# A smaller descriptor area for GpSimd's DMAs in a hybrid attention and Strassen feed-forward layer: 8 KB in place of 16 KB

## Chip, cores, metric

The kernel runs on one core of one Trainium2 chip. The metric is the device time of one execution in microseconds (us); the median of a few runs is given. A profiled execution has a span (first to last instruction) that is a little shorter than its device time.

## What is computed

One layer of a streaming encoder on x of 2048 rows by 1024 columns, float32:

```
h = rmsnorm(x, ln1_w);  proj = h @ w_in
o_diff = diff_attention(dq, dk, dv, lam, ...)    # 4 heads, 128-row query blocks, chunk-causal
o_hgrn = hgrn2(hq, hf, hi, hg, lb, ...)          # 4 heads, chunks of 64 rows, a state is carried
x = x + concat([o_diff, o_hgrn]) @ w_out         # 1024 x 1024
x = x + (silu(conv3(u)) * v) @ w_down            # u, v = rmsnorm(x, ln2_w) @ w_up, width 2816
```

## The kernel before

All matrix products with weights are made from halves: an operand is split into a rounded high part and the rest, and three matmuls (high by high, high by low, low by high) are summed in PSUM. The program has four stages.

**Mixer** (to L530). Four passes s over heads, one attention head and one HGRN head in each; a pass walks over eight blocks b of 256 rows. The steps of a block (projections, attention, HGRN) are written out by the string ORDER. Attention of a 128-row query block (`attn`, L350) goes over the keys in segments of up to 1024 for two components c: scores `sc` (L368, L369) on TensorE (PE), the row maximum `nm` (L376) on VectorE (DVE), the exponential `p` (L387) on ScalarE (ACT). There is one `sc` buffer, so the next scores wait for the exponential before. `attn_o` (L396) combines the two components (L414, DVE), transposes p (`tpa`, L420), copies it (`aT`, L422) and multiplies by the values (`av`, L425). HGRN (`hgrn`, L436) has seven levels, each with a matmul `lt` (L454) between DVE operations. A result of 128 rows goes to DRAM: `od` from `oo` (L434, attention) or from `o` (L499, HGRN). The last pass ends with the attention of query blocks 14 and 15 and the HGRN of the last 256 rows, with no projection left beside them.

**Output projection** (L533 to L626). First w_out is loaded in eight slices of 128 rows (`raw`, L546), rounded (`wo`, L548, ACT) and its rest computed (L549, GpSimd for even slices, DVE for odd). Then 16 tiles i of 128 rows: `load_o` loads the mixer's rows `ot` (L556) and x (`xt`, L558), transposes `ot` on PE (`tpo`, L564) and splits it (`oT`: L569 ACT, L570 DVE); 48 matmuls make `pjo` in two halves of 24 (L613 to L615); `xt` is added (L616), stored (L617), normalized (L620 to L622) into `ht`, which `tail` transposes (`tph`, L582) and scales for the next stage:

```
WO = []
for kt in range(ND):
    raw = rw.tile([P, D], F32, name="raw", tag="raw")
    dma(out=raw, in_=w_out[kt * P:(kt + 1) * P, :])
    w = wp.tile([P, 2, D], F32R, name=f"wo{kt}")
    ACT.copy(w[:, 0], raw)
    (POOL if kt in WOP else DVE).tensor_tensor(out=w[:, 1], in0=raw, ...)
...
def load_o(i):
    ot = wk.tile([P, D], F32, name="ot", tag="ot")
    dma(out=ot, in_=o_d[i])
```

**Up** (L633 to L736) and **down** (L739 to L881) are the two products of the feed-forward part, each by Strassen-Winograd with seven products of half size. In the down stage the partial sums of three of four groups are added to `x2d` in DRAM by accumulating DMAs that GpSimd issues (L830), 48 in all; all other DMAs are issued by SyncE's queue (SP).

**What sets the order.** The code above is traced once; a scheduler at compile time then writes a fixed order for each engine, and every engine and the SP queue carry theirs out strictly in it, waiting on semaphores. A tile may be given out only when what lay at its place is released. So the place of the buffers decides which instructions may be moved ahead of which.

**Where the buffers lie.** Each partition has one stack of pools from the bottom and one from the top. At the bottom lies the descriptor area of GpSimd's DMAs (16,384 bytes), then constants and the raw buffers `rw`, up to byte 35,840. The mixer's pool `wp` (w_in, 57,344 bytes) lies from there to 93,184; of its pools from the top the lowest is `hp` (two `hT` of 16,384 bytes, 94,208 to 126,976), above it `pp` and `sm` (small statistics, from 133,120). The next stage starts again at 35,840: `wp2` (eight `wo` of 8,192 bytes, 65,536) to 101,376, then `wk2` (`ot`, two `xt`, four `oT`, `ht`; 32,768 bytes) to 134,144. So the eighth `wo` and `ot` lie on `hT`, `oT` and `ht` on `hT` and `pp`, and the end of `ht` on the statistics of `sm`, which attention uses to its end.

The function that the diff touches:

## Time and profile before

| | before |
|---|---|
| median of 3 runs (lowest, highest) | 2782.8 us (2782.5, 2784.72) |
| profiled execution: its own time | 2783.16 us |
| its span; mean granted clock of PE | 2781.4 us; 0.985 |
| PE busy (matmul) | 2650.1 us, 95% |
| DVE, ACT, GpSimd (POOL) busy | 1900.0, 1263.6, 1051.6 us |
| DMA issued by GpSimd (q0) | 25.17 MB in 6912 packets |

Busy time is the union of an engine's instructions; matmuls overlap each other, so the distance from one start to the next says more of their cost than their duration. "Idle before" is the time for which an engine had nothing to run, put down to the instruction whose end let it go on. [...]

### The profile page before, as it was taken

The page shows a single profiled execution, that of the slowest core. Times are in us where ns is not written, and L with a number is a line of the kernel's source. Part 1 is how long each engine was busy: PE and PEld are TensorE (multiplying, and loading weights), DVE is VectorE, ACT ScalarE, POOL GpSimd, SP SyncE. Part 2 cuts the span into 40 slices and gives each one's busy share as a digit, 9 for nine tenths or more (in the row PEclk, how much of TensorE's full clock was granted, in tenths as well). Part 3 has the DMA queues.
Part 4 walks back from the last instruction along what each step waited for, and adds up shares of the span by engine and source line. Part 5 has one row for each costly group of instructions (what it writes and reads, how often), then busy time and mean ns, then how long its engine had stood idle before and what let it go on. Part 6 is the DMA issues. An engine that isn't in the chain of part 4 may idle for free. (4 is left out here: it accounts for less than half of the span.)

```text
span 2781.4 us, 42701 instructions
## 1 busy us (share of the span) xinstructions
PE 2650.1 (95%) x14722; PEld 2305.0 (83%) x14722; DVE 1900.0 (68%) x4058; ACT 1263.6 (45%) x3095; POOL 1051.6 (38%) x1168
## 2 busy tenths in 40 slices
PE   7998999999999999969999999999999998899999
PEld 6888899989999999958887888887888886687887
DVE  4677756676568656762327666669777778977787
ACT  4555644564456445542334434445344344434332
POOL 3221222212222222220325334433443446887775
PEclk9999999999999999979999999999999999999999
DMA  5323422242223232124765222225222224775754
GB/s 183 118 106 111 131 85 88 80 131 86 85 84 96 98 115 78 30 64 156 237 205 157 84 76 91 84 76 185 81 91 75 85 91 119 166 163 132 178 172 169
DMA packets 273492, 322.92 MB, mean 116 GB/s; under 512 B 19470, under 2 KB 238974, under 8 KB 269182
## 3 DMA queue, kind: packets, MB, share of 16 engines
q1 hardware_dynamic: 266366, 295.04, 32.4%
q0 software_dynamic: 6912, 25.17, 5.3%
q8 instruction: 117, 1.92, 0.3%
q14 instruction: 97, 0.79, 0.1%
HBM read 198.50 MB, written 104.86 MB: 109 GB/s over the span
## 5 line engine op out<-in xcount | busy, mean ns | idle before, releaser
L697 PE MATMUL q<-xT,WS 128*128 128x512 f32 x704 | 274.5, 390 | 2.6 <-ACT xT L630 2.6
L698 PE MATMUL q<-xT,WS 128*128 128x512 f32 x704 | 274.8, 390 | 2.2 <-DVE xT L631 2.1
L699 PE MATMUL q<-xT,WS 128*128 128x512 f32 x704 | 274.4, 390 | 0.0
L811 PE MATMUL pd<-TW,SG 128*128 128x512 f32 x616 | 244.9, 398 | 19.7 <-DVE acc L817 6.4
L813 PE MATMUL pd<-TW,SG 128*128 128x512 f32 x616 | 242.7, 395 | 3.3 <-DVE SG L631 3.3
L812 PE MATMUL pd<-TW,SG 128*128 128x512 f32 x616 | 244.0, 396 | 1.0 <-DVE TW L631 0.7
L630 ACT CAST WS<-st 128x512 fp32r<-128x512 f32 x176 | 108.5, 618 | 245.0 <-PE q L699 230.3
L697 PE MATMUL q<-xB,WS 128*128 128x512 f32 x528 | 206.9, 392 | 1.3 <-ACT xB L630 1.3
L698 PE MATMUL q<-xB,WS 128*128 128x512 f32 x528 | 206.8, 392 | 1.4 <-DVE xB L631 1.4
L699 PE MATMUL q<-xB,WS 128*128 128x512 f32 x528 | 206.6, 392 | 0.9 <-DVE WS L631 0.9
L387 ACT ACTIVATE p<-sc,nm 128x1024 f32<-128x1024 f32 (+4 forms) x192 | 165.5, 862 | 72.5 <-DVE nm L376 71.3
L631 POOL TENSOR_TENSOR WS<-st,WS 128x512 fp32r<-128x512 f32 x44 | 87.8, 1997 | 281.4 <-ACT WS L630 274.6
L376 DVE TENSOR_REDUCE nm<-sc 128x1 f32<-128x1024 f32 (+4 forms) x192 | 173.9, 906 | 12.7 <-PE sc L369 10.8
L258 PE MATMUL pj<-WA,hT 128*128 128x384 f32 x512 | 177.3, 346 | 2.6 <-DVE hT L245 2.6
L260 PE MATMUL pj<-WA,hT 128*128 128x384 f32 x512 | 175.2, 342 | 0.0
L259 PE MATMUL pj<-WA,hT 128*128 128x384 f32 x512 | 174.9, 342 | 0.0
L425 PE MATMUL av<-vst,aT 128*128 128x128 f32 x1088 | 153.0, 283 | 7.6 <-ACT aT L422 7.2
L811 PEld LDWEIGHTS pd<-TW,SG 128*128 128x128 f32 x616 | 117.9, 192 | 50.0 <-DVE acc L817 7.7
L698 PEld LDWEIGHTS q<-xT,WS 128*128 128x128 f32 x704 | 132.4, 188 | 31.1 <-DVE xT L631 3.6
L697 PEld LDWEIGHTS q<-xT,WS 128*128 128x128 f32 x704 | 132.4, 188 | 30.6 <-ACT xT L630 3.1
L630 ACT CAST WS<-rawu 128x512 fp32r<-128x512 f32 x132 | 82.2, 624 | 164.2 <-PE q L699 163.6
L699 PEld LDWEIGHTS q<-xT,WS 128*128 128x128 f32 x704 | 132.4, 188 | 27.3
(415 smaller groups left out, 7889.5 us busy)
## 6 DMA issues: line engine op xcount, KB each, us to landing
hT<-hTd SPq DMA_DIRECT2D x24, 2048.0 KB, 7.8
rawu<-in_w_up_dram SPq DMA_DIRECT2D x176, 256.0 KB, 3.0
x2d<-acc POOLq DMA_DIRECT2D x48, 512.0 KB, 6.4
gd<-c SPq DMA_DIRECT2D x176, 128.0 KB, 1.9
G<-gd SPq DMA_DIRECT2D x24, 768.0 KB, 4.2
hTd<-hT SPq DMA_DIRECT2D x8, 2048.0 KB, 6.2
qT<-qh SPq DMA_DIRECT2D x256, 64.0 KB, 2.0
rawd<-in_w_down_dram SPq DMA_DIRECT2D x22, 512.0 KB, 4.1
```

The lines of the kernel that those rows point to most:

```text
L258: PE.matmul(dst, lhsT=lh, rhs=rh, start=dt == 0, stop=False)
L259: PE.matmul(dst, lhsT=lh, rhs=rl, start=False, stop=False)
L260: PE.matmul(dst, lhsT=ll, rhs=rh, start=False, stop=dt == ND - 1)
L376: DVE.tensor_reduce(out=nm, in_=sc[:, 0:w], axis=AX.X, op=ALU.max, negate=True)
L387: ACT.activation(out=p[:, 0:w], in_=sc[:, 0:w], func=AF.Exp, bias=nm, accum_out=l)
L630: ACT.copy(dst[:, 0], src)
L697: PE.matmul(dst, lhsT=w[:, 0, cs], rhs=b_[:, 0, dt], start=dt == 0, stop=False)
L698: PE.matmul(dst, lhsT=w[:, 0, cs], rhs=b_[:, 1, dt], start=False, stop=False)
L699: PE.matmul(dst, lhsT=w[:, 1, cs], rhs=b_[:, 0, dt], start=False, stop=dt == 3)
L811: PE.matmul(pd, lhsT=Sx[n][:, 0, k], rhs=w[:, 0], start=k == 0, stop=False)
L812: PE.matmul(pd, lhsT=Sx[n][:, 0, k], rhs=w[:, 1], start=False, stop=False)
L813: PE.matmul(pd, lhsT=Sx[n][:, 1, k], rhs=w[:, 0], start=False, stop=k == len(qs) - 1)
```

## The change

The program is made with a descriptor area of 8,192 bytes per partition in place of 16,384:

```
-    nc = bacc.Bacc("TRN2", target_bir_lowering=False, num_devices=1)
+    nc = bacc.Bacc("TRN2", target_bir_lowering=False, num_devices=1, dynamic_dma_scratch_size=8192)
```

Everything that stands on the bottom stack moves down by 8,192 bytes; what hangs from the top stays. The mixer's `wp` now ends at 84,992. `wp2` is 27,648 to 93,184: its eighth slice lies in the gap below `hT` (84,992 to 93,184), which the mixer does not use. `wk2` is 93,184 to 125,952 and lies on the two `hT` alone. No instruction is added or removed, but the scheduler writes another order for the end of the mixer; ahead of it, and from the `pjo` matmuls of tile 1 on (but for four of the eight `tph` of tile 0, which come ahead of them), the order is the same.

**SP queue, end of the mixer's last pass.** `od` are the mixer's stores, `raw` the slices of w_out, `ot` and `xt` the inputs of an output tile (od_97 are the rows of tile 0, od_98 those of tile 1). Before:

```order
L434 DMA od_109<-oo 128x128
L546 DMA raw<-in_w_out_dram 128x1024 x2
L499 DMA od_109<-o_16457 128x128
L546 DMA raw<-in_w_out_dram 128x1024 x2
...
L434 DMA od_111<-oo 128x128
L499 DMA od_111<-o_16803 128x128
L499 DMA od_112<-o_16826 128x128
L434 DMA od_112<-oo 128x128
L556 DMA ot<-od_97 128x1024
L558 DMA xt<-in_x_dram 128x1024 x2
L556 DMA ot<-od_98 128x1024
```

Now:

```order
L434 DMA od_109<-oo 128x128
L556 DMA ot<-od_97 128x1024
L558 DMA xt<-in_x_dram 128x1024
L546 DMA raw<-in_w_out_dram 128x1024
L558 DMA xt<-in_x_dram 128x1024
L546 DMA raw<-in_w_out_dram 128x1024
L499 DMA od_109<-o_16457 128x128
L546 DMA raw<-in_w_out_dram 128x1024
L556 DMA ot<-od_98 128x1024
L434 DMA od_110<-oo 128x128
L546 DMA raw<-in_w_out_dram 128x1024
```

The inputs of tiles 0 and 1 have moved from behind the mixer's last store to places among the last loads of w_out.

**PE, last HGRN levels and scores.** `wo_16874` is the slice wo0 of w_out, `wo_16889` wo3 and `wo_16894` wo4. Before:

```order
L454 MATMUL lt<-qP,kp 128x128 x2
L368 MATMUL sc<-kst,qT 128x512
L369 MATMUL sc<-kst,qT 128x512
L368 MATMUL sc<-kst,qT 128x512
L369 MATMUL sc<-kst,qT 128x512
L454 MATMUL lt<-qP,kp 128x128 x2
```

Now, from the second `lt` of these on:

```order
L454 MATMUL lt<-qP,kp 128x128
L613 MATMUL pjo<-wo_16889,oT 128x512
L614 MATMUL pjo<-wo_16889,oT 128x512
L615 MATMUL pjo<-wo_16889,oT 128x512
L613 MATMUL pjo<-wo_16894,oT 128x512
L368 MATMUL sc<-kst,qT 128x512
L369 MATMUL sc<-kst,qT 128x512
L368 MATMUL sc<-kst,qT 128x512
L369 MATMUL sc<-kst,qT 128x512
L614 MATMUL pjo<-wo_16894,oT 128x512
L615 MATMUL pjo<-wo_16894,oT 128x512
```

All 48 `pjo` matmuls of tile 0 (9 ahead of that `lt`, these, and so on), its 8 `tpo` and the 8 of tile 1 have moved ahead of the last `av` matmuls of the mixer, between scores, levels and transposes.

**ACT, the eighth slice.** `wo_16909` is wo7. The difference on ACT at that place:

```order
 L548 CAST wo_16904<-raw 128x1024
-L548 CAST wo_16909<-raw 128x1024
+L569 CAST oT<-tpo 128x512 x2
 L381 ACTIVATE wv<-nm,nm_16522 128x1
 L387 ACTIVATE p,l<-sc,nm_16522 128x896
+L548 CAST wo_16909<-raw 128x1024
```

The rounding of wo7 has moved behind one exponential, and the split of tile 0's `oT` stands in its place; on DVE the rest of wo7 (L549) has moved behind one row maximum in the same way.

## Rows read from the trace of the kernel before

**Rows 1.** The page, part 2: busy and granted clock in 40 slices.

```profile
PE   7998999999999999969999999999999998899999
PEclk9999999999999999979999999999999999999999
```

**Rows 2.** Stretches: length, busy per engine (x instructions), PEclk, DMA share, GB/s.

```profile
1190.00:1212.00 22.00, 11.80 (x55) 8.88 (x54) 20.37 (x43) 12.19 (x24) 10.48 (x10) 0.73 0.51 152
1212.00:1246.00 34.00, 24.31 (x135) 20.70 (x135) 19.34 (x56) 12.64 (x33) 4.13 (x6) 0.77 0.03 7
1246.00:1254.00 8.00, 1.97 (x8) 1.57 (x8) 0.96 (x3) 0.96 (x4) 0.74 (x2) 0.62 0.59 203
1254.00:1268.00 14.00, 13.40 (x52) 10.76 (x52) 2.32 (x4) 0.63 (x2) 0.00 (x0) 0.85 0.12 39
```

**Rows 3.** PE in order of time: start, length, engine, operation, [idle before, releaser].

```profile
1211.13 0.63 PE L454 MATMUL lt<-qP,kp 128*128 128x128 f32 x2
...
1214.58 0.80 PE L368 MATMUL sc<-kst,qT 128*128 128x512 f32 x1
...
1219.54 0.50 PE L368 MATMUL sc<-kst,qT 128*128 128x512 f32 x1 [0.23 <-ACT p L387]
...
1229.40 0.50 PE L368 MATMUL sc<-kst,qT 128*128 128x512 f32 x1
...
1238.15 1.94 PE L420 MATMUL tpa<-ident,p 128*128 128x128 f32 x8 [1.71 <-DVE p L414]
...
1243.61 2.05 PE L425 MATMUL av<-vst,aT 128*128 128x128 f32 x16 [0.24 <-ACT aT L422]
1251.78 1.97 PE L564 MATMUL tpo<-ident,ot 128*128 128x128 f32 x8 [6.12 <-DMA ot<-od]
...
1254.89 0.63 PE L614 MATMUL pjo<-wo,oT 128*128 128x512 f32 x1
1255.32 0.63 PE L615 MATMUL pjo<-wo,oT 128*128 128x512 f32 x1
...
1258.47 0.40 PE L614 MATMUL pjo<-wo,oT 128*128 128x512 f32 x1
1258.70 0.39 PE L615 MATMUL pjo<-wo,oT 128*128 128x512 f32 x1
...
1268.46 0.47 PE L613 MATMUL pjo<-wo,oT 128*128 128x512 f32 x1
...
1280.37 1.03 PE L564 MATMUL tpo<-ident,ot 128*128 128x128 f32 x8
```

**Rows 4.** SP queue in order of time, end of the mixer.

```profile
1183.35 0.33 SPq L434 DMA_DIRECT2D od<-oo  x1
...
1197.79 4.14 SPq L546 DMA_DIRECT2D raw<-in_w_out_dram  x2
...
1248.10 0.42 SPq L556 DMA_DIRECT2D ot<-od  x1
```

**Rows 5.** ACT (first two rows) and DVE in order of time.

```profile
1205.49 1.04 ACT L548 CAST wo<-raw 128x1024 fp32r<-128x1024 f32 x1 [2.03 <-DMA raw<-in_w_out_dram]
...
1208.34 0.99 ACT L387 ACTIVATE p<-sc,nm 128x896 f32<-128x896 f32 x1
...
1210.24 1.20 DVE L549 TENSOR_TENSOR wo<-raw,wo 128x1024 fp32r<-128x1024 f32 x1
...
1217.03 1.22 DVE L376 TENSOR_REDUCE nm<-sc 128x1 f32<-128x1024 f32 x1
```

**Rows 6.** GpSimd's DMAs: parts 3 and 6, its costliest lines, one stretch.

```profile
q0 software_dynamic: 6912, 25.17, 5.3%
...
x2d<-acc POOLq DMA_DIRECT2D x48, 512.0 KB, 6.4
...
L830 POOL DMA_DIRECT2D x2d<-acc x48 | 46.8, 1035 | 9.1 <-POOL acc L817 6.2 <-DVE acc L817 2.9
...
2351.00:2676.00 325.00, 310.16 (x1325) 251.41 (x1324) 271.12 (x338) 126.77 (x265) 257.38 (x220) 0.98 0.67 155
```

## Prediction

> **What bounds the kernel now.** I read the page in slices first: PE is at nine tenths or more in nearly all of the 40, and where it is, only less matmul work would save time. The diff leaves the work alone, so a gain can only come from slices in which PE is not full. One such dip (6, with the granted clock at 7) is the 18th slice, 1182 to 1251 us [rows 1], and there lies the only place where the order differs. Then I read that place in stretches [rows 2]: from 1190 to 1212 PE is busy for 11.80 of 22 us while DVE is busy for 20.37; from 1212 to 1246 PE has 34.00 - 24.31 = 9.69 us of idle; from 1246 to 1254 it works for 1.97 of 8 us. The granted clock is below 1 in all of them. Last, in order of time [rows 3]: the mixer's tail is a chain from engine to engine (scores, maximum, exponential, scores) with PE waiting in between. The mixer's last `av` matmuls end at 1243.61 + 2.05 = 1245.66. Then PE stands for 6.12 us, until `ot` of tile 0 has landed, which SP issued only at 1248.10, behind the last store [rows 4]. Tile 0 follows alone, its first matmuls at half clock: one each 0.43 us (1254.89, 1255.32), from 1258.47 on one each 0.23 us (1258.47, 1258.70). Tile 1's matmuls begin at 1268.46, and from then on PE is full. So 1268.46 - 1245.66 = 22.80 us lie between the mixer's last matmul and the first of tile 1, with nothing but tile 0 in them.
>
> **The change, part by part.** *The area itself.* No instruction goes or comes. GpSimd's 48 accumulating stores make 6912 packets, or 6912 / 48 / 16 = 9 per DMA engine and store. A store takes 6.4 us to land, and its issue holds GpSimd for 1.035 us on average [rows 6]. The 48 fall in 325 us, 6.8 us apart on average and in pairs, so some two to four are in flight, 18 to 36 packets per engine. The trace does not show how many the area holds. I take the cost as nothing; the other end is the ring rival below. [...]
>
> *The addresses.* The mixer's code and the up and down stages keep their order, and I know of no row that makes the cost of a buffer depend on where it lies: nothing.
>
> *Tile 0's loads* go out behind the store at 1183.35 [rows 4] in place of 1248.10. Three more transfers of 512 KB (tile 0's two inputs and tile 1's `xt`) share the engines before 1200, tile 1's `ot` follows after that; the DMA share of 1190 to 1212 was 0.51 [rows 2], so there is room. What they could make late is the last slice of w_out. Its load is the second of the two that SP issued from 1197.79 on, and ACT waited 2.03 us for it and rounded it at 1205.49 [rows 5]. In the new order that rounding stands behind the exponential of 1208.34, which ends at 1209.33 [rows 5], so the load may land 1209.33 - 1205.49 = 3.8 us later at no cost. On DVE the rest of this slice (1.20 us at 1210.24 [rows 5]) moves behind the next maximum, and tile 0's `oT` takes its place.
>
> *PE's moved work.* Ahead of the mixer's end PE now has 48 `pjo` and 16 `tpo` more. At 0.23 us each and 1.03 us for eight transposes [rows 3] this is 48 x 0.23 + 2 x 1.03 = 13.1 us; at the low clock (0.43, and 1.97 for eight) it is 24.6 us. The idle time from 1212 to 1246 covers 9.69 us, and each matmul stands in PE's order ahead of something of the mixer, so the tail must become later somewhere. I walk it by its checkpoints, taking the low clock for as much as ran at it after 1251.78, eight transposes and some nine matmuls ((1258.47 - 1254.89) / 0.43 and one more), here a dozen matmuls for the gaps between them, and the full one then.
>
> 1. The level matmuls of 1211.13 are unchanged. Nine `pjo` at 0.43 follow, to 1215.6, then a level, then four more, mostly at 0.43, to about 1217.2. The scores that began at 1214.58 begin there, 2.6 us later. The maximum behind them began at 1217.03 only, since DVE was busy [rows 5]; now it waits for the scores (four at 0.23 us and their drain) and begins at about 1218.5, 1.5 us later.
> 2. The next scores come after that maximum and its exponential at 1221.2 (before: 1219.54), 1.7 late. The `pjo` between them fit into the wait at 0.23 us.
> 3. DVE now carries `xt` + `pjo` of tile 0 (0.7 us) in this part, and transposes and `av` share PE with seven more `pjo`: the fourth scores come at about 1231.3 (before: 1229.40), 1.9 late.
> 4. The last transposes wait for the last combination on DVE: about 1240.0 (before: 1238.15), 1.8 late. They then run at the full clock, since PE has been busy with ten `pjo` and more: eight in 1.03 us and not in 1.94. ACT has the square of tile 0 (about 1.2 us) between the last `aT`, which costs about as much as one of the two sets of transposes saves. The last `av` end at about 1244.8, 0.9 us ahead of 1245.66.
> 5. Tile 0 is done by then, `ot` of tile 1 is there and transposed, so tile 1's matmuls need only four `tph` first and begin at about 1245.4.
>
> So 1268.46 - 1245.4 = 23.1 us go, and 0.4 us more, because four `tph` (half of what eight transposes take, 0.5 us) now lie ahead of that point: 23.5 us. Tile 2's transposes were at 1280.37 [rows 3] and should be at about 1257. Its `ot` is issued once tile 1's last transpose is through, eleven us ahead; it took less than four from 1248.10 to 1251.78, so that wait does not come back. From there on all waits are between instructions that move together, and the whole rest shifts.
>
> The profiled execution took 2783.16 us: 2783.16 - 23.5 = 2759.7. The median of the runs is 0.4 us lower, so I say 2759.3 us. The bounds: if the tail ends 4 us earlier than walked (no checkpoint late, and the full clock through), 2755.5; the upper end is the first rival.
>
> **The rivals.** *The clock stays low through the tail.* The 35 `pjo` and 16 `tpo` that I took at full clock would cost 35 x 0.20 + 2 x 0.94 = 8.9 us more, at most all of it on the path: 2759.3 + 8.9 = 2768.2. For it: the clock was 0.73 and 0.77 in these stretches [rows 2]. Against it: PE was idle for (22.00 - 11.80) + 9.69 = 19.9 of 56 us there, and now would hardly be; after 1251.78 it rose once PE was kept at work. [...]
>
> *The change brings nothing.* PE's idle time could be only moved: the tail late by as much as tile 0 brings forward, 2782.8. For it: PE's order is strict, and `pjo` now stands ahead of scores; if one slice of w_out were late by 20 us, everything behind it would be. Against it: at the low clock throughout, and with no cover but the idle time after 1212, the tail is late by 24.6 - 9.69 = 14.9 us, less than the 22.8 that go. Only late weights can do it, and the last slice is rounded at 1205.49 [rows 5], far ahead of that.
>
> *The smaller area makes GpSimd wait (slower).* If a store held GpSimd until the area had room, at worst until the store before had landed, each of 48 would hold it 6.4 us in place of 1.035, 258 us in all. In these 325 us GpSimd is busy for 257.38, so 67.6 us are free [rows 6], and the rest, 190 us, would fall on the stage: 2759.3 + 190 = 2949. It ends slower than before once a hold exceeds (67.6 + 23.5) / 48 = 1.9 us. For it: GpSimd makes the sums that PE's products read, at 79% busy. Against it: two to four in flight in an area of thousands of bytes.
>
> **How the numbers follow.** Forecast (gain 19 to 27 us) 0.76; low clock or other lateness in the tail (gain 6 to 19) 0.17; nothing 0.03; GpSimd waits 0.04. A measurement of this kernel tells about 0.2% from no change, 5.6 us. Faster: 0.93; same: 0.03; slower: 0.04. The range runs from the lower bound, 2755.5, to just over the low-clock rival, 2769.
>
> **What would show it.** Right: the first `tpo` near 1192 and the first `pjo` near 1212; PE busy for all but a few of the us from 1212 to 1246; the last `av` within 3 us of 1245; no wait of 6 us for `ot`; tile 2's transposes near 1257; the stages after it as long as before; the 48 stores at about 1.0 us each. Wrong: low clock from 1216 to 1240, a wait of `pjo` for `wo`, a wait of scores longer than 3 us, or stores that hold GpSimd for longer than before.

## The result and the profile after

The changed kernel took 2755.6 us (median of the first executions), the kernel before 2783.6 us beside it: ratio 0.9896, 95% interval 0.9877 to 0.9916. The forecast was 2759.3 us and the range 2755.5 to 2769.0; 0.9896 of the 2783.16 us on which the sum was made is 2754.2, just below the lower end. (One of these first executions took 6136.55 us; nothing like it came back in any later run, and it is not in the ratio.) Measured once more in the first experiment, the same kernel has a ratio of 0.9912 (0.9892 to 0.9932), and 0.9912 x 2783.16 = 2758.7 lies inside. So the first two medians are 28.0 us apart, outside the gain of 19 to 27 us that had most of the weight, and the second measurement gives 24.5. The profiled execution took 2755.53 us, span 2753.7.

The page in slices, as in [rows 1]:

```profile
PE   7999999999999999989999999999999998899999
PEclk9999999999999999999999999999999999999999
```

The 6 of the 18th slice, with its 7 of clock, is gone; an 8 stands there, with a 9 of clock. The stretches of [rows 2] (length, busy time of PE, PEld, DVE, ACT, POOL, then granted clock as a share of full speed, DMA share, GB/s):

```profile
1190.00:1212.00 22.00, 13.76 (x57) 10.62 (x56) 19.45 (x44) 11.28 (x22) 9.89 (x9) 0.69 0.53 163
1212.00:1246.00 34.00, 32.16 (x201) 27.05 (x200) 20.99 (x54) 14.65 (x38) 3.69 (x10) 1.00 0.19 62
1246.00:1254.00 8.00, 8.00 (x42) 6.61 (x41) 1.37 (x2) 1.38 (x5) 0.00 (x0) 1.00 0.12 36
1254.00:1268.00 14.00, 13.76 (x73) 11.47 (x72) 4.49 (x8) 5.22 (x15) 0.74 (x2) 1.00 0.57 188
```

From 1212 on PE is idle for 1.84 us of 34 (before 9.69), and the granted clock is 1.00. The first stretch is much as before: at 0.69 (before 0.73), and idle for more than 8 us of 22. TensorE in order of time, as in [rows 3]:

```profile
1188.03 0.66 PE L564 MATMUL tpo<-ident,ot 128*128 128x128 f32 x4 [0.37 <-DVE qk L347]
...
1194.04 0.38 PE L476 MATMUL op<-ones,qk 128*128 128x1 f32 x2 [2.01 <-DVE st L493]
...
1206.90 0.63 PE L454 MATMUL lt<-qP,kp 128*128 128x128 f32 x2
1207.18 0.77 PE L613 MATMUL pjo<-wo,oT 128*128 128x512 f32 x1
1207.75 0.63 PE L614 MATMUL pjo<-wo,oT 128*128 128x512 f32 x1
...
1210.70 0.40 PE L615 MATMUL pjo<-wo,oT 128*128 128x512 f32 x1
1210.94 0.38 PE L454 MATMUL lt<-qP,kp 128*128 128x128 f32 x2
...
1212.09 0.39 PE L368 MATMUL sc<-kst,qT 128*128 128x512 f32 x1
...
1225.75 0.48 PE L368 MATMUL sc<-kst,qT 128*128 128x512 f32 x1
...
1234.80 1.07 PE L420 MATMUL tpa<-ident,p 128*128 128x128 f32 x8 [1.12 <-DVE p L414]
...
1239.28 2.05 PE L425 MATMUL av<-vst,aT 128*128 128x128 f32 x16
...
1241.63 0.48 PE L613 MATMUL pjo<-wo,oT 128*128 128x512 f32 x1
...
1253.13 1.03 PE L564 MATMUL tpo<-ident,ot 128*128 128x128 f32 x8
```

The last `av` end at 1239.28 + 2.05 = 1241.33 and tile 1's `pjo` start 0.30 us later; before, 22.80 us lay between them. The wait of 6.12 us for `ot` is gone, since SP now issues that load at 1179.85:

```profile
1179.48 0.33 SPq L434 DMA_DIRECT2D od<-oo  x1
1179.85 0.44 SPq L556 DMA_DIRECT2D ot<-od  x1
```

All of this execution is early, though, already ahead of the first place where the order differs: the store of 1179.48, behind which the new order starts on SP, is the one of 1183.35 before [rows 4], 3.87 us later. The HGRN matmul `op` (L476) that began at 1194.04 is the one that began here in the kernel before:

```profile
1197.92 0.38 PE L476 MATMUL op<-ones,qk 128*128 128x1 f32 x2 [2.33 <-DVE st L493]
```

It waits for DVE in both, and the seven `tpo` of tile 0 that now stand ahead of it on PE left the offset as it was: 3.88 us. So this much of the gain of this pair of executions comes from work that the change does not touch. I take this `op` as a checkpoint below and split every execution there.

The signs that the forecast named came: on the clock of before the first `tpo` is at 1188.03 + 3.88 = 1191.9 (near 1192), the first `pjo` at 1207.18 + 3.88 = 1211.1 (near 1212).

### The profile page after: what moved, and what is told of

Read it like the earlier page. It is cut to its first block, busy times and chain, and to the rows that moved or that the text cites. A ratio compares the mean times of both kernels' runs of the same rounds, so it can differ in the third digit from the quotient of the medians.

```text
span 2753.7 us, 42698 instructions
## 1 busy us (share of the span) xinstructions
PE 2641.4 (96%) x14722; PEld 2298.5 (83%) x14722; DVE 1897.0 (69%) x4058; ACT 1263.0 (46%) x3095; POOL 1051.1 (38%) x1168
## 5 line engine op out<-in xcount | busy, mean ns | idle before, releaser
L697 PE MATMUL q<-xT,WS 128*128 128x512 f32 x704 | 274.8, 390 | 2.3 <-ACT xT L630 2.3
L697 PE MATMUL q<-xB,WS 128*128 128x512 f32 x528 | 207.3, 393 | 1.3 <-ACT xB L630 1.2
L697 PEld LDWEIGHTS q<-xT,WS 128*128 128x128 f32 x704 | 132.5, 188 | 30.0 <-ACT xT L630 2.8
```

Of the source, the lines that this page charges most:

```text
L697: PE.matmul(dst, lhsT=w[:, 0, cs], rhs=b_[:, 0, dt], start=dt == 0, stop=False)
```

## Experiments

**The changed kernel once more.** Nothing is edited.

> The changed kernel, unaltered, once more. In the first traces the changed kernel is 3.9 us ahead of the kernel before already at the row maximum that began at 1190.32 before and at 1186.44 after, ahead of every place where the order differs. Theory A (chance: a low clock near 276 us and slices of w_in that land later fall differently from one execution to the next): the time is 2753 to 2757 us, and that row maximum may begin anywhere from 1186 to 1190. Theory B (the smaller area or the lower addresses speed up the mixer): it begins within 0.5 us of 1186.4 again.

Measured: ratio 0.9912 (0.9892 to 0.9932). Its executions took 2751.41 to 2762.78 us, those of the kernel before on the same chip 2777.76 to 2791.17, far wider than the three on which the forecast rests (2782.5 to 2784.72). In its trace the row maximum begins at 1189.41, not near 1186.4, which is theory A:

```profile
1189.41 1.21 DVE L376 TENSOR_REDUCE nm<-sc 128x1 f32<-128x1024 f32 x1
```

The median, 2759.73, is above the 2753 to 2757 that I gave to that theory; the kernel before was at 2784.47 on this chip.

**The smaller area alone.** 8 KB of padding behind the area; every place and every order as before.

```
-    few.tile([P, FEW // 4], F32, name="pad")
+    few.tile([P, FEW // 4], F32, name="pad"); few.tile([P, 2048], F32, name="pad8")
```

> The area of 8 KB with 8 KB of unused padding behind it: every buffer lies where it lay before and the order on every engine is that of before; only the area is smaller. If the tail's new order makes the gain and A holds: 2783.6 us, within 1.5. If the smaller area itself gives the 4 us ahead of the tail: 2779.6. If the smaller area makes GpSimd's stores wait (the rival on the slower side): above 2785, with the 48 stores holding GpSimd for more than 1.2 us each.

Measured: 1.0002 (0.9988 to 1.0015). The area itself neither costs nor gives anything that can be measured.

**The weights' own place alone.** The padding stands between the slices of w_out and the pool of the output tiles.

```
-        wk = pool(ms, "wk2", 1)
+        pool(ms, "gap2", 1).tile([P, 2048], F32, name="pad8"); wk = pool(ms, "wk2", 1)
```

> The area of 8 KB, the mixer's pools on the left and all of w_out's slices where they lie after the change (the eighth in its own place), but 8 KB of padding below the pool of the output tiles, so that this pool starts at byte 101376 as before and its end lies on the statistics again. The order on every engine is that of before. If the early loads of tile 0 make the gain: 2783.6 us, within 1.5. If the eighth slice's own place makes a part of it: below 2780. If the mixer's lower addresses give the 4 us (B): 2779.6.

Measured: 0.9994 (0.9982 to 1.0006), the order of before on every engine. Neither the eighth slice's own place nor the mixer's lower addresses are worth anything that can be measured.

**An area of 14 KB.** `dynamic_dma_scratch_size=14336`.

> An area of 14,336 bytes: everything on the left stack moves down by 2 KB only. The eighth slice lies on the first hT again, as before, but the pool of the output tiles ends at byte 132096, below the statistics. The order on every engine is that of the changed kernel. If only the order of the tail counts: 2755 us, within 1.5. If the eighth slice's own place counts, its rounding waits for the release of hT and the time is 2757 to 2760. If the 8 KB area or the lower mixer gives the 4 us (B): 2758 to 2760.

Measured: 0.9908 (0.989 to 0.9926). With the eighth slice on `hT` again, and 2 KB freed in place of 8, the whole gain is there. The median, 2757.73, taken by itself lies in the bands of the rivals; but these were only 2 us away, less than the same kernel differs between executions, and the changed kernel itself was at 2759.73 on this chip. The ratios decide: 0.9908 beside its 0.9912.

**An area of 15 KB.** `dynamic_dma_scratch_size=15360`.

> An area of 15,360 bytes: the left stack moves down by 1 KB only, so that the pool of the output tiles ends at byte 133120, exactly where the statistics begin. The scheduler then moves tile 0 ahead of the mixer's end as in the changed kernel; only the four transposes of its normalized rows and one load stay behind. If all of the gain hangs on that last 1 KB on the statistics (theory of the order): a ratio of 0.991 to before, 2758 to 2760 us. If a good part of it comes from the room that 8 KB leave (the slice's own place, or less sharing): 2765 or more.

Measured: 0.9902 (0.9888 to 0.9916). So 1 KB decides: before, the pool of the output tiles ended 1,024 bytes inside the mixer's statistics, and that overlap alone held tile 0 behind the mixer; with everything else lower and that overlap kept (the run on the weights' own place) nothing was gained.

**An area of 1 KB.** `dynamic_dma_scratch_size=1024`, and 15 KB of padding behind it; order and places of before.

> An area of 1 KB with 15 KB of unused padding behind it: places and order of before. If GpSimd's stores never wait for room even with a sixteenth of the area (two to four stores in flight): a ratio of 1.000 within 0.002, and the stores at 1.0 to 1.15 us each. If the area bounds them (the rival on the slower side): the stores hold GpSimd for 2 us and more each and the ratio is 1.01 to 1.07.

Measured: 0.9997 (0.9986 to 1.0008). The 48 stores of GpSimd (shortest/median/longest in ns, first and last start), first before, then after the change, then with 1 KB:

```profile
L830 POOL DMA_DIRECT2D x2d<-acc x48: 854/1122/1194, 2351.4 to 2675.2; - x48
```

```profile
L830 POOL DMA_DIRECT2D x2d<-acc x48: 868/1046/1217, 2324.2 to 2647.5; - x48
```

```profile
L830 POOL DMA_DIRECT2D x2d<-acc x48: 864/1137/1233, 2349.1 to 2673.1; - x48
```

None holds GpSimd for longer than 1.233 us. The slower rival needed far more: by the prediction's sum, 1.9 us a store on top of the 1.035 of before (the prediction calls the 1.9 the whole hold, but the free time of 67.6 us has the stores' own time already taken off). So no wait for room was seen. How much the area holds, and what GpSimd does when it is full, no run shows.

**Tile 0's `pjo` behind the mixer, its loads ahead.** In PSUM banks that the mixer holds to its end, the sums of tile 0 cannot start early. Nothing is left out.

```
-EARLY, TP, LO, HSB, HVB, XTB = 1, 1, 2, 5, 3, 2
+EARLY, TP, LO, HSB, HVB, XTB = 0, 1, 2, 5, 3, 2
```

> The changed kernel with tile 0's sums in PSUM banks that the mixer holds to its end (EARLY 0 in place of 1): the loads, transposes and splits of tiles 0 and 1 stay ahead of the mixer's end, but all 48 pjo of tile 0 stand behind the last av again. If the gain is made of two parts, the wait for tile 0's inputs (some 9 us from the last av to the first pjo) and the overlap of its pjo (some 14 us), this run has only the first: a ratio of 0.996 to 0.9975, and tile 1's pjo 12 to 14 us behind the last av. If the early loads alone are what counts: 0.991. If they bring nothing without the overlap: 1.000.

Measured: 0.9931 (0.9918 to 0.9943), more than I gave the first part. TensorE in order of time; 1252.23 is the first `pjo` of tile 1:

```profile
1239.45 2.05 PE L425 MATMUL av<-vst,aT 128*128 128x128 f32 x16 [0.24 <-ACT aT L422]
1241.26 0.48 PE L613 MATMUL pjo<-wo,oT 128*128 128x512 f32 x1
1241.57 0.40 PE L614 MATMUL pjo<-wo,oT 128*128 128x512 f32 x1
...
1252.23 0.39 PE L613 MATMUL pjo<-wo,oT 128*128 128x512 f32 x1
```

Tile 0's 48 `pjo` and what lies between them take 1252.23 - 1241.26 = 10.97 us. Before it was 1268.46 - 1254.30 = 14.16, from this row on:

```profile
1254.30 0.79 PE L613 MATMUL pjo<-wo,oT 128*128 128x512 f32 x1 [0.55 <-DVE oT L570]
```

There the first nine ran at half the clock (granted 0.50 from 1248 to 1258) behind the wait for `ot`, and tile 1's eight transposes stood between the last of them and tile 1's `pjo`. I had counted only the wait.

**More raw buffers in the freed space.** Five in place of four; then six with an area of 4 KB; then seven with 1 KB.

```
-RB, QTB, FB, IGB, ATB, KVB, PBB = 4, 3, 2, 4, 3, 5, 6
+RB, QTB, FB, IGB, ATB, KVB, PBB = 5, 3, 2, 4, 3, 5, 6
```

> The changed kernel with a fifth raw buffer of 4 KB out of the freed space, so that slices of w_in and of w_out are loaded one further ahead. In the trace of before, ACT waits 1.8 to 2.4 us for such slices at 308.99, 322.31 and 613.02 us, three waits of the kind in each of three passes. If these waits lie on the path: 4 to 8 us less than the changed kernel, a ratio of 0.988 to 0.990. If they are hidden or come back elsewhere: 0.991 to 0.992, like the changed kernel. The scheduler also writes another order for the mixer (some 1,260 lines on TensorE), so that a loss up to 0.995 is possible.

> An area of 4 KB and six raw buffers in place of four: the same places as in the run with five, but one more slice ahead. Theory of waits for slices: 0.987 to 0.990. Theory that they are hidden: 0.991 to 0.992. If an area of 4 KB makes GpSimd's stores wait, they hold it for more than 1.2 us each and the down stage gets longer than in the changed kernel.

> An area of 1 KB and seven raw buffers in place of four, which takes 12 KB of the 15 KB freed. With five and six buffers the up stage took 847.5 and 845.0 us in place of 856.4, and the ratio was 0.9873 and 0.9867. If the waits for slices are used up: 0.986 to 0.987, the up stage at 843 to 845 us. If each further buffer still gives as much as the sixth did: 0.9855 to 0.986. If GpSimd's stores wait in an area of 1 KB once they meet more loads: stores above 1.2 us each.

Measured: 0.9873 (0.9859 to 0.9886), 0.9867 (0.9853 to 0.988) and 0.9862 (0.9847 to 0.9877): all three below the 0.9892 at which the interval of the changed kernel in the first experiment begins, and not to be told apart from each other. With 1 KB and seven buffers no store held GpSimd for longer than 1.227 us. ACT's waits for slices of w_in (us, times) fell as expected; after the change:

```profile
  DMA raw<-in_w_in_dram: 7.0, 9
```

and with six buffers:

```profile
  DMA raw<-in_w_in_dram: 1.2, 2
```

The ratios are near those that I gave to waits on the path (0.987 to 0.990 with five or six), but not for that reason: the mixer got no faster. Its `op` (see above) begins at 1194.00, 1196.84 and 1196.61 with five, six and seven buffers, and between 1191.74 and 1197.92 with four. Most of the gain came where I had not looked, in the up stage, whose loads use the same buffers. The stage as one stretch, after the change and with six buffers:

```profile
1434.40:2291.00 856.60, 845.86 (x3703) 696.83 (x3703) 611.92 (x728) 361.86 (x584) 353.84 (x230) 0.99 0.31 97
```

```profile
1439.50:2284.50 845.00, 840.82 (x3703) 694.83 (x3703) 621.52 (x728) 359.64 (x584) 354.87 (x230) 1.00 0.32 99
```

11.6 us less: 6.6 us of PE's idle time (10.74 to 4.18) and 5.0 us of its busy time, at a clock of 1.00 and not 0.99 on average. This is no chance of one pair: from the first to the last start of its L697 matmuls on `xT` the stage takes 843.2 to 846.5 us in the nine traces with four raw buffers and 836.5, 834.9 and 834.3 in those with five, six and seven. 3.8 us of the idle time that goes stood ahead of products whose right-hand sides had just been loaded and split; after the change and with six buffers:

```profile
L697 PE MATMUL q<-xT,WS 128*128 128x512 f32 x696 | 271.7, 390 | 2.3 <-ACT xT L630 2.3
L698 PE MATMUL q<-xT,WS 128*128 128x512 f32 x695 | 271.6, 391 | 2.3 <-DVE xT L631 2.2
```

```profile
L698 PE MATMUL q<-xT,WS 128*128 128x512 f32 x701 | 273.5, 390 | 0.7 <-DVE xT L631 0.7
L697 PE MATMUL q<-xT,WS 128*128 128x512 f32 x701 | 273.4, 390 | 0.0
```

## Why the prediction was nearly right, and where it failed

The traced executions with four raw buffers, split at the `op` that began at 1197.92 before and at 1194.04 after. The columns are worked out from the traces: the start of `op`; from there to the end of the last `av`, to tile 1's first `pjo`, to tile 2's first `pjo`, and to the end of the span; and the granted clock in the 56 us that begin 7.92 us ahead of `op`.

| kernel | op | last av | tile 1 | tile 2 | end | clock |
|---|---|---|---|---|---|---|
| before | 1197.92 | 47.74 | 70.54 | 83.78 | 1583.4 | 0.76 |
| area alone, its order | 1193.36 | 49.59 | 73.06 | 86.30 | 1583.8 | 0.70 |
| weights' place, its order | 1194.71 | 49.89 | 73.43 | 86.66 | 1587.3 | 0.70 |
| area of 1 KB, its order | 1193.51 | 49.43 | 72.70 | 85.93 | 1585.5 | 0.70 |
| after | 1194.04 | 47.29 | 47.59 | 60.36 | 1559.6 | 0.88 |
| after, again | 1197.01 | 46.50 | 46.81 | 59.57 | 1557.8 | 0.88 |
| area of 14 KB, order of after | 1194.36 | 47.28 | 47.58 | 60.32 | 1559.5 | 0.88 |
| area of 15 KB, order of after but for four transposes and a load | 1191.74 | 47.68 | 47.54 | 60.76 | 1557.5 | 0.85 |
| pjo late | 1193.15 | 48.35 | 59.08 | 71.65 | 1568.3 | 0.76 |

*The mechanism: right, and shown.* The gain is the new order of the tail. The runs with the order of before are at 1.000 wherever their buffers lie, those with the order of after (in the run with 15 KB but for four transposes and a load) at 0.9896 to 0.9912 whatever the area. The smaller area and the weights' own place, which the section on the change describes, do nothing by themselves; what the new order needed was 1 KB. The addresses at no cost and the area at no cost, both taken in the sum, hold.

*The walk of the tail: its end right to 0.4 us, by two errors that cancel.* With the 3.88 us of offset added, after's rows are on the clock of before: the scores of 1212.09 at 1215.97 (walked 1217.2, before 1214.58), those of 1225.75 at 1229.63 (1231.3, before 1229.40), the last transposes of 1234.80 at 1238.68 (1240.0, before 1238.15), the last `av` end at 1245.21 (1244.8, before 1245.66), tile 1's `pjo` at 1245.51 (1245.4), tile 2's `tpo` at 1257.01 (1257).

The first error made the checkpoints late. Nine `pjo` do stand where I had put them, behind the level matmuls that began at 1211.13 before and at 1206.90 after, and the first eight came 0.44 us apart. But they began 0.28 us behind the start of that level, where I had let it end first (0.63), and from 1210.70 on one came each 0.24 us, so that the next level and the four `pjo` behind it took 1212.09 - 1210.94 = 1.15 us and not 1.6. Much of this lay in a wait of PE for DVE; this is that next level before:

```profile
1213.70 0.77 PE L454 MATMUL lt<-qP,kp 128*128 128x128 f32 x2 [1.94 <-DVE kp L451]
```

The scores came 1.4 us later than before and not 2.6, and the maximum behind them, for which DVE had not been free before until 1217.03 [rows 5], came at 1213.21 + 3.88 = 1217.09 and not at 1218.5:

```profile
1213.21 1.23 DVE L376 TENSOR_REDUCE nm<-sc 128x1 f32<-128x1024 f32 x1 [0.43 <-PE sc L369]
```

So each checkpoint was 1.2 to 1.7 us ahead of the walk. The second error gave it back: from the last transposes to the end of the last `av` the walk has 1244.8 - 1240.0 = 4.8 us, and the run took 1241.33 - 1234.80 = 6.53. Step 4's own terms give 6.6: before it was 1245.66 - 1238.15 = 7.51, and one set of transposes at the full clock saves 0.9. The step took this 0.9 off 1245.66 and left out the 1.8 us by which it had the transposes late. Added up by its own terms the walk ends at 1246.6, its gain is 21.7 and the forecast 2761.1 us. That 23.5 meets this pair's gain behind the checkpoint, 83.78 - 60.36 = 23.4, is luck.

*The split of the gain was off.* The run with `pjo` late divides it. To tile 2's first `pjo`, the mean of the four with the order of before is 85.7 and that of the three with all of the order of after 60.1: 85.7 - 71.65 = 14.0 us come with the early loads and transposes, 71.65 - 60.1 = 11.6 with tile 0's `pjo` inside the tail. To the end it is 1585.0 - 1568.3 = 16.7 and 1568.3 - 1559.0 = 9.3, and by the ratio, 0.9931, the first part is 19. Only one execution with late `pjo` was traced, so the split is known to a few us; the first part is in each case more than the 9 that I gave it (and 14 to the second). The wait cost more than its 6.12 us: behind it the first nine `pjo` ran at the low clock (granted 0.50 from 1248 to 1258, and 0.62 on average from 1246 to 1254 [rows 2]), while with late `pjo` and no such wait it was 1.00 over the 22 us from 1241.23 on.

*The step that failed: the bounds, and one execution taken as the kernel.* The lower bound, 2755.5, was a single term, "if the tail ends 4 us earlier than walked"; the part "the mixer's code and the up and down stages keep their order: nothing" put at nothing whatever differs outside the tail, and the sum was made against one execution of before. In the first pair the tail did not end 4 us earlier than walked but 0.4 later; what passed the bound is time of work that nobody touched, which differs from execution to execution. Of the 27.7 us between the two first spans 3.9 lie ahead of the checkpoint, 23.4 from there to tile 2's first `pjo` and 0.4 behind it. The 3.9 alone were enough to carry the time past a bound that was 3.8 below the forecast, and they are not the change's as far as can be seen: the starts of `op` in the table lie between 1191.74 and 1197.92, with means of 1194.9 in the order of before and 1195.1 in the three with all of that of after. Behind the checkpoint the term of 23.5 was too small: the execution I walked was the quickest of four with its order to tile 2's first `pjo` (83.78; the others 85.93 to 86.66), at a clock of 0.76 and not 0.70. On the means the gain there is 85.7 - 60.1 = 25.6 us, and 1585.0 - 1559.0 = 26.0 to the end. The three executions on record, 2782.5 to 2784.72, did not show such a spread; the 23 of the first experiment do, at 6.7 us on either side of their median.

*The rivals.* The clock that stays low: not so; in the execution after it is 0.50 from 1197.0 to 1210.6 and 1.00 from 1210.7 to 1246.0. The longest stretch at 0.50 in the trace of before runs from 1200.2 to 1217.1, with PE busy for 9.78 of these 16.9 us. Nothing gained: not so. GpSimd waiting for room (the ring rival): not so, down to 1 KB, where no store held it for longer than 1.233 us; that the area has room for the 18 to 36 packets per engine was my estimate, and how much it holds no run shows.

## What to carry to other kernels

Where buffers share memory in turn, list for each what lies at its place before and when that is released: here a pool that ended 1 KB inside something long-lived held the start of a whole stage behind it, and the size of the cure says nothing about the size of the gain. Then move only that edge, and look for what the rest of the freed space buys: here raw buffers gave another 0.3 to 0.5%. Make the sum against several executions, or widen the bounds by the waits and low clocks that are chance in the one at hand.

## What the runs showed of the hardware

The same order on every engine ran the same 56 us of the tail at a granted clock of 0.76 in one execution and 0.70 in three, whose last `av` ended 1.7 to 2.2 us later behind `op` (the table above). Executions of the kernel before spread over 2777.76 to 2793.71 us. Those with more raw buffers lie closer together, 2747.08 to 2750.61, 2744.88 to 2748.74 and 2742.87 to 2747.41 us, though there are only four of each; what the spread of the others comes from was not shown. An area of 1 KB served the 48 accumulating stores as well as one of 16 KB: a ratio of 0.9997, and GpSimd held for a median of 1137 ns a store beside 1122.
